# A decoder trunk whose first products take raw transposed tokens, the row norm applied at eviction

## The chip, the cores and the metric

The kernel runs on one core of one Trainium2 chip. The core has a matrix engine (TensorE, PE in the profile, with its weight loads as PEld), a vector engine (VectorE, DVE), a scalar engine (ScalarE, ACT), GpSimd (POOL) and a queue engine (SyncE, SP) that issues most of the DMAs. The metric is the device time of one execution in microseconds; lower is better. The time shown for a kernel is the median of several runs.

## The reference

A trunk of two pre-norm layers on 256 tokens of width 1024, all in float32. In each layer the RMS-normalised tokens go through one wide input projection, whose columns feed three causal mixers (a Mamba-2 scan, a sliding-window attention with sinks, a forgetting attention). Each mixer's output is projected, weighted by a sigmoid gate, summed, projected again and added to the stream. A last RMSNorm closes the trunk.

```
def rms_norm(x, w):
    y = x * lax.rsqrt(jnp.mean(x * x, axis=-1, keepdims=True) + NORM_EPS)
    return y * w

for layer in range(2):
    h = rms_norm(x, norm_w[layer])
    proj = h @ w_in[layer]            # 12832 columns
    (a_xbc, a_z, a_dt, b_q, b_k, b_v, b_z, c_q, c_k, c_v, c_f, c_z, gates) = split(proj)
    y_a = mamba2_branch(a_xbc, a_z, a_dt, ...)
    y_b = sliding_window_branch(b_q, b_k, b_v, b_z, sinks[layer], cos, sin)
    y_c = forgetting_attention_branch(c_q, c_k, c_v, c_f, c_z, f_bias[layer])
    branch = [y_a @ w_proj[layer, 0], y_b @ w_proj[layer, 1], y_c @ w_proj[layer, 2]]
    merged = sum(sigmoid(gates_i + gate_bias[layer, i]) * branch[i])
    x = x + merged @ w_out[layer]
return rms_norm(x, final_norm_w)
```

Note that a row's factor rsqrt(mean(x²)+eps) is one number per token. It can be applied to the tokens before a product or to the product's rows after it.

## The kernel before

**Products.** TensorE's fast float32 form takes rounded operands, so each operand is split: a high part (a rounded copy, written by ScalarE) and a low part (the remainder, original minus high, usually by VectorE). Every product is three passes: high by high, low by high, high by low (`dense`, line 273). The tokens are kept transposed as `hTh` and `hTl`, [128, 2 row tiles of 128 tokens, 8 slices of the width, 128].

**Weights.** The weight matrices are cut into pieces (256 or 512 columns) and these into parts of 512 KB, in one stream. `load_to` (line 327) issues the DMAs of parts on SP into six `raw` buffers. `feed` (line 358) splits parts, up to four ahead of the product in hand (`AHEAD`), into six `hi` and six `lo` buffers; `release` calls it as a product finishes with a part. One narrow piece of 32 columns (dt and the forget gate) has a buffer of its own.

**Order.** `ops` is a list of operations written out by hand. Layer 0 starts with k and v of the window attention (256 columns each, two parts each), then two q pieces of 512 columns (four parts each), then the narrow piece, the gate piece z, and the convolution pieces ("heavy") with lighter ones between (`lights`): two c_v pieces, gates, output projections. Attention and scan work is launched as generators with a delay in estimated TensorE time, and `pump` puts ready steps between products; `drain` forces one branch's steps out. TensorE runs in the written order throughout (`manual_schedule`). In the first section of the program, up to the v products, VectorE, ScalarE and GpSimd do as well; behind it a planner orders those engines. SP's queue is ordered by the planner too; `pin` keeps an instruction in written order on its engine.

**Banks.** Wide products take three banks (`pmm`), the rest, transposes among them, five (`pmx`).

**The start** (lines 1134 to 1181). SP loads x rows 0-127, the norm weight copied to all partitions, x rows 128-255, and the parts; GpSimd loads the rope table. Thirty transposes of the identity occupy TensorE (`WARM`). For the first row tile the squares are summed, the row factor is made (`row_rstd`: GpSimd's power and four small VectorE steps), x is multiplied by factor and weight (line 1160), transposed and split (`to_hT`). The second row tile goes through GpSimd and ScalarE and is transposed in the middle of the first k product (`second_rows`, through `after`). Two parts are split in halves by ScalarE with VectorE or GpSimd taking the remainder (lines 1148 and 1149).

**The constants** of a layer (`layer_consts`, line 403) are nine small DMAs in layer 0, issued on ScalarE's queue after the v products.

**The end** (`out_end`, line 988). For the last columns: add the residual (VectorE), square and sum (ScalarE), multiply by the final norm weight (VectorE), add to the variance (line 1003), power on GpSimd, two small VectorE steps, and then VectorE scales columns 0 to 511 and ScalarE 512 to 1023, each followed by its own DMA.

Of the kernel before, what the change touches and what calls it, by code (L numbers as in the profile page):

```python
# [16 lines left out]
P = 128  # L17
# [12 lines left out]
N_RAW, N_SPLIT = 6, 6  # L30
AHEAD = 4
WARM = 30
# [11 lines left out]
def hybrid_trunk(  # L44
# [110 lines left out]

    tab = T("tab", [P, 1])
# [3 lines left out]
    nwb0 = T("nwb", [P, D])  # L160
    nc.sync.dma_start(x0[:, 0, :], x2[0:P, :])
    nc.sync.dma_start(nwb0, norm_w[0:1, :].to_broadcast([P, D]))
    nc.sync.dma_start(x0[:, 1, :], x2[P:S, :])
# [26 lines left out]
    nc.gpsimd.dma_start(rope_sb, rope_tab.rearrange("(t p) c d -> p t c d", p=P))  # L190
# [82 lines left out]
    def dense(pt, ah, al, bh, bl, w, after=None, mid=None):  # L273


        passes = ((ah, bh), (al, bh), (ah, bl))
# [4 lines left out]
        for i, (k, a, b) in enumerate(seq):  # L281
            mm(pt, a(k), b(k), start=(i == 0), stop=(i == len(seq) - 1))
            if after is not None:
                if i % 12 == 11:
                    after[i // 12]()
# [28 lines left out]
    raws, pieces, pieces_out = {}, {}, {}  # L314

# [11 lines left out]
    def load_to(j):  # L327

        while state["load"] < min(j, len(stream)):
            i, k = stream[state["load"]]  # L330
            src, n = subs[i]
            kper = min(NK, 1024 // n)
            raw = T("raw" if n > 32 else "L1", [P, kper, n])
            for c, ap in src:
                m = ap.shape[-1]
                nc.sync.dma_start(raw[:, :, c:c + m],
                                  ap.rearrange("(k p) c -> p k c", p=P)[:, k:k + kper, :])
            raws[state["load"]] = raw
            state["load"] += 1
# [59 lines left out]
    y0.nwb = nwb0  # L399

    pdma = pin(nc.scalar.dma_start)

    def layer_consts(y):
        l = y.l
        vr = T("vr", [88, P])
# [36 lines left out]
    def tok(ah, al, w, t, turn=True, mid=None, **kw):  # L442
# [3 lines left out]
        p = pmm()  # L446
# [13 lines left out]
    def rope(p, t):  # L460

        p4 = p.rearrange("p (h d) -> p h d", h=4)
        cos = bc(rope_sb[:, t, 0, :], 1, 4)
        a = T("L1", [P, 4, 64])
        tt(a, p4, cos, op=ALU.mult)
        b = T("L1", [P, 4, 64])
        tt(b[:, :, 0:32], p4[:, :, 32:64], bc(rope_sb[:, t, 1, 0:32], 1, 4), op=ALU.mult)
        tt(b[:, :, 32:64], p4[:, :, 0:32], bc(rope_sb[:, t, 1, 32:64], 1, 4), op=ALU.mult)
        return a, b

    def u_bkv(y, c0, t, after=None):

        def f(w):
            p = tok(y.hTh, y.hTl, w, t, turn=w.n == 512 or c0 > 0, after=after)
            if t == 0 and c0 == 0:
                kv = T("L8", [P, 2048])
                y.kT = kv[:, 0:1024].rearrange("p (h s) -> p h s", h=4)
                y.bv = kv[:, 1024:1536].rearrange("p (t c) -> p t c", t=2)
            if c0 > 0:
                act(halves(y.bv[:, t, :]), p, AF.Copy)  # L480
            elif w.n == 512:
                act(y.bv[:, t, :], p[:, 1, :], AF.Copy)
            if c0 == 0:
                a, b = rope(p if w.n == 256 else p[:, 0, :], t)
# [3 lines left out]
                launch(1, rest(kd), D_K)  # L488
# [10 lines left out]
    def u_bq(y, c0, t):  # L499

        def f(w):
            p = tok(y.hTh, y.hTl, w, t, turn=w.n == 512)
            for i in range(w.n // 256):
                if t == 0:
                    y.qT[c0 + i] = T("qt", [P, 2, S])
                a, b = rope(p if w.n == 256 else p[:, i, :], t)
                q = T("L1", [P, 4, 64])
                gtt(q, a, b, op=ALU.add)
                launch(1, rest(c0 + i, q.rearrange("p h d -> p (h d)")), D_Q)
# [90 lines left out]
    def swa_quad(y, c, qT):  # L600
        yield lambda: (1, 0) in y.zdone
# [220 lines left out]
    def u_cv(y, c, t):  # L822
        def f(w):
# [3 lines left out]
            act(halves(y.cv[:, t, c:c + w.n]), p, AF.Copy)  # L827
# [160 lines left out]
    def out_end(y, c, t, i, n, xo, p):  # L988
        sl = slice(c, c + n)
        with tc.high_priority():  # L990
            tt(halves(y.xn[:, t, sl]), p, halves(xo), op=ALU.add)
            sum_sq(y.xn, t, c, y.ss[t][:, i:i + 1], n)
            last = y.l + 1 == L
            nwb = fin["w"] if last else layers[y.l + 1].nwb
            if last:
                stt(y.xn[:, t, sl], y.xn[:, t, sl], -0.5, nwb[:, sl], op0=ALU.mult, op1=ALU.mult)
# [4 lines left out]
            if i == 2:  # L1001
                v = y.var[t][:, 1:2]
                stt(v, y.ss[t][:, 2:3], 1.0 / D, y.var[t][:, 0:1], op0=ALU.mult, op1=ALU.add)
                r = row_rsqrt2(v)
                if last:
                    ts(y.xn[:, t, 0:512], y.xn[:, t, 0:512], r[:, 0:1], None, op0=ALU.mult)
                    nc.sync.dma_start(out2[t * P:(t + 1) * P, 0:512], y.xn[:, t, 0:512])
                    act(y.xn[:, t, 512:D], y.xn[:, t, 512:D], AF.Copy, scale=r[:, 0:1])  # L1008
                    nc.scalar.dma_start(out2[t * P:(t + 1) * P, 512:D], y.xn[:, t, 512:D])
# [34 lines left out]
    for y in layers:  # L1044
        l = y.l
        w = w_in[l]
        y.gate, y.qT, y.ckT, y.sz, y.yh, y.yl, y.sq, y.h, y.ss, y.var, y.zdone, y.cqdone = {}, {}, {}, {}, {}, {}, [], {}, {}, {}, set(), {}
# [11 lines left out]
        def gates_proj(br):  # L1059
# [4 lines left out]
            def p(b):  # L1064
                c = 512 * b
                if b == 0 and br != 0:
# [34 lines left out]
        lights = [lambda: None, lambda: op(cols(C_CV, 512), u_cv(y, 0, 0), u_cv(y, 0, 1))]  # L1101
        lights += [lambda: None, lambda: op(cols(C_CV + 512, 512), u_cv(y, 512, 0), u_cv(y, 512, 1))]
# [114 lines left out]
```

## Time and profile before

| | before |
|---|---|
| median of 3 runs | 848.63 us (848.49 to 848.87) |
| profiled execution, its time | 847.65 us |
| its span, first to last instruction | 845.9 us |
| mean granted TensorE clock | 0.996 |
| TensorE busy | 833.4 us, 99% |
| VectorE busy | 642.3 us, 76% |
| ScalarE busy | 511.6 us, 60% |

The span is shorter than the time by 1.75 us, which lies around the first and last instruction. Rows of a timeline read: start, duration, engine, line, operation, what it writes and reads with shapes, a count, and in brackets the engine's idle time just before and what ended it. The chain of work is followed back from the last instruction; its rows are start, duration and what it was. Rows of waits read: who waited for whom, total us, times, longest. Rows by window read: the stretch, its length, then busy us and count of PE, PEld, DVE, ACT and POOL, the granted clock as a share of full speed, the DMA engines' busy share, and GB/s. A TensorE row that counts as busy can still run at a lower clock.

### The profile page before, as it was taken

The numbers are of one execution on the slowest core, as the hardware profiler recorded it, in microseconds if no ns is written. First come the engines' busy times: TensorE is split into PE (matmuls) and PEld (weight loads), VectorE is DVE, ScalarE is ACT, GpSimd is POOL, SyncE is SP. The second block draws the span as 40 slices with busy tenths as digits, with TensorE's granted clock in tenths as the row PEclk, the third lists the DMA queues.
The fourth block names the chain that finished last, engine by engine and source line by source line (L and its number), as shares of the span: only waits on it lengthen the run. The fifth ranks groups of instructions, "written<-read, shape, count | busy, mean of one in ns | idle before, by whom it ended". The sixth has DMA issues, their size and how long they took to land.

```text
span 845.9 us, 15985 instructions
## 1 busy us (share of the span) xinstructions
PE 833.4 (99%) x5964; PEld 763.3 (90%) x5964; DVE 642.3 (76%) x1403; ACT 511.6 (60%) x1004; POOL 104.5 (12%) x134
## 2 busy tenths in 40 slices
PE   7999999999999999999999999999999999999996
PEld 7999898989999998888989998899899999988896
DVE  5777997998776679656788879879968667785665
ACT  6466777665666667435555667776557667654442
POOL 6310100000131010210014001000003110121000
PEclk9999999999999999999999999999999999999999
DMA  8666565666465545648676465465755555576632
GB/s 303 183 205 208 166 200 162 201 210 197 128 202 175 172 159 187 218 155 282 206 237 218 143 206 159 142 199 183 241 171 176 174 175 152 161 235 212 212 100 76
DMA packets 126638, 158.43 MB, mean 187 GB/s; under 512 B 12784, under 2 KB 88224, under 8 KB 126560
## 3 DMA queue, kind: packets, MB, share of 16 engines
q1 hardware_dynamic: 109456, 140.79, 52.9%
q10 hardware_dynamic: 17056, 16.49, 6.4%
q8 instruction: 47, 0.77, 0.4%
q14 instruction: 31, 0.25, 0.1%
q0 software_dynamic: 48, 0.13, 0.0%
HBM read 155.22 MB, written 2.16 MB: 186 GB/s over the span
## 4 chain that ended last, share of the span: by engine, by line
PE 95%; DMA 2%; ACT 0%; DVE 0%; issue 0%; POOL 0%; SPq 0%; POOLq 0%; DVEq 0%; ACTq 0%
PE mm L96 82%; PE mx L96 9%; PE mx L100 4%; DMA raw<-in_w_proj_dram 2%; DMA raw<-in_w_in_dram 1%; POOL lo L1149 0%; ACT hi L1148 0%; ACT hi L259 0%; ACT L L1008 0%; DVE L L260 0%; DVE L L935 0%; DVE L L934 0%; ACT L L259 0%; POOLq L1213 0%; ACT L L215 0%
## 5 line engine op out<-in xcount | busy, mean ns | idle before, releaser
L260 DVE TENSOR_TENSOR lo<-raw,hi 128x1024 fp32r<-128x1024 f32 x252 | 308.2, 1234 | 94.9 <-ACT hi L259 81.9
L96 PE MATMUL mm<-hi,L 128*128 128x512 f32 (+1 forms) x1344 | 373.9, 364 | 1.9 <-ACT hi L1148 1.4
L259 ACT ACTIVATE hi<-raw 128x1024 fp32r<-128x1024 f32 x252 | 263.2, 1056 | 93.0 <-PE mm L96 66.9
L96 PE MATMUL mm<-L,hi 128*128 128x256 f32 x1792 | 317.7, 278 | 0.0
L96 PEld LDWEIGHTS mm<-L,hi 128*128 128x128 f32 x1792 | 277.7, 192 | 6.8 <-issue 3.3
L96 PEld LDWEIGHTS mm<-hi,L 128*128 128x128 f32 x1344 | 241.5, 190 | 32.4 <-issue 2.7
L96 PE MATMUL mm<-L,lo 128*128 128x256 f32 x896 | 246.4, 275 | 0.0
L96 PE MATMUL mm<-lo,L 128*128 128x512 f32 (+1 forms) x672 | 241.3, 360 | 0.6 <-POOL lo L1149 0.6
L96 PEld LDWEIGHTS mm<-L,lo 128*128 128x128 f32 x896 | 171.9, 192 | 0.2
L96 PEld LDWEIGHTS mm<-lo,L 128*128 128x128 f32 x672 | 127.3, 190 | 15.4 <-POOL lo L1149 0.8
L862 POOL TENSOR_SCALAR_AFFINE_SELECT bias<-bias 128x128 f32<-128x128 f32 x64 | 35.7, 593 | 407.8 <-DMA bias<-cumd 232.7
L556 ACT ACTIVATE pp<-pp,nm 128x128 f32<-128x128 f32 (+1 forms) x128 | 56.5, 443 | 13.0 <-DVE nm L550 13.0
L693 DVE SCALAR_TENSOR_TENSOR L<-L,vec,L 128x255 f32<-128x255 f32 (+2 forms) x96 | 46.3, 482 | 4.8 <-ACT L L690 3.4
L96 PE MATMUL mx<-L,L 128*64 128x128 f32 (+1 forms) x384 | 34.4, 314 | 0.0
L886 ACT ACTIVATE L<-L 128x512 f32<-128x512 f32 x24 | 15.2, 632 | 30.2 <-DVE L L885 30.0
L568 DVE TENSOR_SCALAR pp<-pp,rsum 128x128 f32<-128x128 f32 (+1 forms) x128 | 32.1, 314 | 0.5
L696 ACT ACTIVATE L<-L 128x256 f32<-128x256 f32 x32 | 13.3, 417 | 31.4 <-DVE L L693 25.9
L96 PEld LDWEIGHTS mx<-L,L 128*64 128x64 f32 x384 | 22.9, 136 | 9.4 <-ACT pp L556 1.3
L777 ACT ACTIVATE L<-mm 128x256 f32<-128x256 f32 x48 | 18.1, 378 | 21.0 <-PE mm L96 21.0
L585 ACT ACTIVATE L<-mx 128x512 f32<-128x512 f32 x48 | 27.0, 596 | 2.7 <-PE mx L100 2.5
L100 PE MATMUL mx<-ident,pp 128*128 128x128 f32 x192 | 26.3, 273 | 0.0
L100 PE MATMUL mx<-ident,L 128*128 128x128 f32 x152 | 23.1, 279 | 1.6 <-DVE L L935 0.8
(173 smaller groups left out, 716.0 us busy)
## 6 DMA issues: line engine op xcount, KB each, us to landing
raw<-in_w_in_dram SPq DMA_DIRECT2D x200, 512.0 KB, 4.3
raw<-in_w_proj_dram SPq DMA_DIRECT2D x48, 512.0 KB, 5.6
raw<-in_w_out_dram SPq DMA_DIRECT2D x16, 512.0 KB, 5.1
L<-cumd ACTq DMA_DIRECT2D x8, 512.0 KB, 5.2
bias<-cumd ACTq DMA_DIRECT2D x16, 256.0 KB, 3.8
L<-in_gate_bias_dram ACTq DMA_DIRECT2D x12, 256.0 KB, 3.9
L<-in_x_dram SPq DMA_DIRECT2D x2, 512.0 KB, 5.0
nwb<-in_norm_w_dram SPq DMA_DIRECT2D x1, 512.0 KB, 5.4
```

The lines of the kernel that those rows point to most:

```text
L96: nc.tensor.matmul(o, a, b, **kw)
L100: nc.tensor.transpose(o, a, i)
L259: keep(act)(hi, src, AF.Copy)
L260: keep(tt)(lo, src, hi.bitcast(F32), op=ALU.subtract)
L556: act(pp[:, i, sl], pp[:, i, sl], AF.Exp, scale=-1.0, bias=nm[:, e:e + 1], accum_out=sums[:, e:e + 1])
L568: ts(pp[:, i, sl], pp[:, i, sl], rs[:, 2 * i + b:2 * i + b + 1], 0.5, op0=ALU.mult, op1=ALU.mult)
L585: act(pT, pt, AF.Copy)
L693: stt(a[:, s:S], x_[:, 0:S - s], y.vec[:, 16 * j + u:16 * j + u + 1], a[:, s:S], op0=ALU.mult, op1=ALU.add)
L696: act(th, a, AF.Tanh)
L777: act(halves(th), p, AF.Tanh, scale=0.5)
L862: nc.gpsimd.affine_select(out=bias[:, i, dst], in_=bias[:, i, src], compare_op=ALU.is_ge, fill=NEG, base=0, pattern=[[-1, P]], channel_mul ...
L886: act(g, g, AF.Tanh, scale=0.5)
```

## The change

In layer 0 the first products (k, v, both q pieces and the first c_v piece) take x transposed and multiplied by the norm weight, without the row factor. The factor is applied where these products leave their banks: in the rope steps of k and q, and as the scale of the copies of v and c_v. The norm weight arrives as an [8, 128] block on ScalarE's queue and is transposed once, instead of the copy to all partitions.

The k evictions are kept back (`late`) until after the v products, since the factor exists only then; the first k tile gets a bank from the other pool. After the q pieces a new step `normalize` broadcasts the factor by two small products and multiplies the stored transposed tokens by it, splitting them into new `hTh` and `hTl`, which everything from the narrow piece on uses. For this the first c_v piece moves ahead of the narrow piece; the lighter pieces between the heavy ones are placed anew in layer 0, and the split of the window attention's output is placed two operations earlier.

SP's queue is reordered: x rows 0-127 in two halves, part 0 in two halves, part 1, x rows 128-255, the rope table (from GpSimd's queue), then parts 2 to 5. The constants of layer 0 are issued by SP when the stream reaches part 8, no longer by ScalarE. The narrow piece is loaded when the stream is eight parts short of it, in both layers. The thirty transposes at the start become ten, with ten more before the first product.

At the end of the last layer the last squares are summed on VectorE, the variance step comes ahead of the multiplication by the norm weight, and the last scaling is divided at column 640.

```diff
-WARM = 30
+EARLY = 8
+WARM = 10
+FILL = 10
...
+    nw8 = T("L1", [NK, P])
+    nc.scalar.dma_start(nw8, norm_w[0:1, :].rearrange("o (k p) -> (o k) p", p=P))
...
-    nc.sync.dma_start(x0[:, 0, :], x2[0:P, :])
-    nc.sync.dma_start(nwb0, norm_w[0:1, :].to_broadcast([P, D]))
-    nc.sync.dma_start(x0[:, 1, :], x2[P:S, :])
+    for j in range(2):
+        nc.sync.dma_start(x0[:, 0, j * 512:(j + 1) * 512], x2[0:P, j * 512:(j + 1) * 512])
...
+    def load_part(j):
+        i, k = stream[j]
+        ...
+        step_ = kper // 2 if j == 0 else kper
+        ...
+    def load_to(n_):
+        while state["load"] < min(n_, len(stream)):
+            j = state["load"]
+            for e in range(j, min(j + EARLY, len(stream))):
+                if subs[stream[e][0]][1] == 32 and e not in raws and e >= state["split"]:
+                    load_part(e)
+            if j == 8:
+                layer_consts(y0, nc.sync)
+            if j not in raws:
+                load_part(j)
+            state["load"] += 1
...
+        for o, i, r in ((a, p4, rope_sb[:, t, 0, :]),
+                        (b[:, :, 0:32], p4[:, :, 32:64], rope_sb[:, t, 1, 0:32]),
+                        (b[:, :, 32:64], p4[:, :, 0:32], rope_sb[:, t, 1, 32:64])):
+            if y.rn is None:
+                tt(o, i, bc(r, 1, 4), op=ALU.mult)
+            else:
+                stt(o, i, y.rn[:, t:t + 1], bc(r, 1, 4), op0=ALU.mult, op1=ALU.mult)
...
-            p = tok(y.hTh, y.hTl, w, t, turn=w.n == 512 or c0 > 0, after=after)
+            p = tok(y.hTh, y.hTl, w, t, turn=w.n == 512 or c0 > 0, after=after,
+                    bank=pmx if after and t == 0 else pmm)
+            end()
...
+            (late.append if after is not None else lambda g: g())(lambda: evict(w, p))
...
-                act(halves(y.bv[:, t, :]), p, AF.Copy)
+                act(halves(y.bv[:, t, :]), p, AF.Copy, scale=y.rn[:, t:t + 1])
...
-            sum_sq(y.xn, t, c, y.ss[t][:, i:i + 1], n)
+            if last and i == 2:
+                nc.vector.tensor_tensor_reduce(out=junk[:, 0:n], in0=y.xn[:, t, sl], in1=y.xn[:, t, sl], ...)
+            else:
+                sum_sq(y.xn, t, c, y.ss[t][:, i:i + 1], n)
+            if i == 2:
+                v = y.var[t][:, 1:2]
+                pin(stt)(v, y.ss[t][:, 2:3], 1.0 / D, y.var[t][:, 0:1], op0=ALU.mult, op1=ALU.add)
             if last:
-                stt(y.xn[:, t, sl], y.xn[:, t, sl], -0.5, nwb[:, sl], op0=ALU.mult, op1=ALU.mult)
+                pin(stt)(y.xn[:, t, sl], y.xn[:, t, sl], -0.5, nwb[:, sl], op0=ALU.mult, op1=ALU.mult)
...
+                    m = 640
...
-            op(k, u_bkv(y, 0, 0, [lambda j=j: second_rows(j) for j in range(2)]))
-            op(k, u_bkv(y, 0, 1))
+            op(k, u_bkv(y, 0, 0, {16: lambda: second_rows(0), 20: lambda: second_rows(1)}, lambda: first_end()))
+            op(k, u_bkv(y, 0, 1, {}))
             op(v, u_bkv(y, 256, 0), u_bkv(y, 256, 1))
-            op(None, lambda: layer_consts(y0))
             for c in (0, 2):
                 op(cols(C_BQ + 256 * c, 512), u_bq(y, c, 0), u_bq(y, c, 1))
+            op(None, lambda: launch(9, normalize(y0), 0.0))
+            op(cols(C_CV, 512), u_cv(y, 0, 0), u_cv(y, 0, 1))
+            op(None, lambda: normalized(y0))
...
+        if l == 0:
+            lights = {2: [lambda: cv(512)], 4: [gp.pop(0)], 6: [lambda: op(None, lambda y=y: split_late(y, 1))],
+                      7: [gp.pop(0)]}
+        else:
+            lights = {1: [lambda: cv(0)], 3: [lambda: cv(512)], 4: [gp.pop(0)], 6: [gp.pop(0)]}
...
+    def normalize(y):
+        rb = T("L1", [P, S])
+        for t in range(2):
+            act(rb[:, t * P:(t + 1) * P], ident, AF.Copy, scale=y.rn[:, t:t + 1])
+        yield 2.0
+        p = pmx()
+        for t in range(2):
+            mm(p[:, t * P:(t + 1) * P], ones, rb[:, t * P:(t + 1) * P], start=True, stop=True)
+        hTh = T("L8", [P, 2, NK, P], F32R)
+        hTl = T("L8", [P, 2, NK, P], F32R)
+        for t in range(2):
+            for k in (0, 4):
+                xk = xw[:, t, k:k + 4, :]
+                tt(xk, xk, bc(p[:, t * P:(t + 1) * P], 1, 4), op=ALU.mult)
+                split(hTh[:, t, k:k + 4, :], hTl[:, t, k:k + 4, :], xk)
...
+        load_to(2)
+        nc.sync.dma_start(x0[:, 1, :], x2[P:S, :])
+        nc.sync.dma_start(rope_sb, rope_tab.rearrange("(t p) c d -> p t c d", p=P))
         load_to(N_RAW)
...
+        square(0, 0)
+        turn(0, 0)
+        w_high(parts[0], 0)
+        high(0, 0)
+        turn(0, 1)
+        for i in range(FILL):
+            transpose(warm[:, 0:P], ident, ident)
+        low(0, 0)
+        w_high(parts[0], 2)
+        w_low(parts[0], 0)
+        w_low(parts[0], 2, gtt)
+        high(0, 1)
+        w_high(parts[1], 0)
+        low(0, 1)
+        w_low(parts[1], 0)
+        w_high(parts[1], 2)
+        w_low(parts[1], 2, gtt)
+        square(0, 1)
+
+        def second_rows(j):
+            turn(1, j)
+
+        def first_end():
+            high(1, 0)
+            high(1, 1)
+            low(1, 0)
+            low(1, 1)
+            w_high(parts[2], 0)
+            w_high(parts[2], 2)
+            w_low(parts[2], 2, gtt)
+            w_low(parts[2], 0)
+            w_high(parts[3], 0)
+            w_high(parts[3], 2)
+            w_low(parts[3], 0)
+            square(1, 0)
+            square(1, 1)
+            w_low(parts[3], 2)
+            ...
+            y0.rn = rsqrt(v, 2)
```

Here `turn` transposes four slices of x and multiplies them by the norm weight (VectorE), `high` and `low` split the tokens (ScalarE, VectorE), `w_high` and `w_low` split half a weight part (`gtt` is GpSimd), and `square` sums squares on ScalarE.

More of the change, by code (lines that the diff above doesn't have):

```diff
@@ new lines, in square @@
+        def square(t, j):
+            sum_sq(x0, t, 512 * j, ss[:, 2 * t + j:2 * t + j + 1], 512)
+        parts = [new_part() for _ in range(4)]
+        square(0, 0)
[12 more added lines that the diff above has]
+        low(0, 1)
@@ L1182, in hybrid_trunk @@
     with tc.manual_schedule(engines={ENG.PE}):
+        for g in late:
+            g()
         for i, f, last in ops[3:]:
```

157 lines of the change are left out of this document (76 added, 81 removed).

## The prediction

> **What bounds the kernel now.** I read the page's busy shares first, then who waited for whom on TensorE, then the chain of work over the first 27 us, then the timelines of both ends.
>
> ```profile
> PE 833.4 (99%) x5964; PEld 763.3 (90%) x5964; DVE 642.3 (76%) x1403; ACT 511.6 (60%) x1004; POOL 104.5 (12%) x134
> PE mm L96 <- ACT hi L1148: 1.4, 1, 1.4
> PE mx L100 <- DVE L L935: 0.8, 1, 0.8
> PE mm L96 <- POOL lo L1149: 0.6, 1, 0.6
> ```
>
> TensorE is busy 99% of 845.9 us. Its longest wait after the start is 0.8 us. Time can be won at the two ends only: before products run densely, and after the last one.
>
> ```profile
> 2.18 7.77 DMA raw<-in_w_in_dram
> 9.98 1.16 ACT hi L1148 x2
> 11.20 1.78 POOL lo L1149
> 13.02 0.80 PE mm L96 x2
> 17.36 8.36 PE mm L96 x72
> ...
> 10.66 1.50 PE L96 MATMUL mm<-hi,L 128*128 128x256 f32 x8 [1.38 <-ACT hi L1148]
> ...
> 25.56 0.60 PE L100 MATMUL mx<-ident,L 128*128 128x128 f32 x4
> ...
> 13.00:16.00 3.00, 2.98 (x14) 2.98 (x15) 0.60 (x2) 1.58 (x4) 2.90 (x2) 0.50 1.06 381
> 16.50:17.00 0.50, 0.50 (x7) 0.50 (x6) 0.50 (x2) 0.43 (x1) 0.00 (x0) 1.00 1.05 389
> ```
>
> The start waits for the first weight part: it lands at 9.95, fourth in SP's queue behind three transfers of 512 KB. Then come its rounding on ScalarE and its remainder on GpSimd. After that sparse stretch the granted clock is 0.50 from 13.0 to about 16.3. The four k and v products end at 25.56 (my mark), where the first q product follows; from there TensorE hardly stops. So the change is worth what it moves this mark, plus the tail, plus new waits.
>
> **The start, step by step.** These rows give the durations:
>
> ```profile
> 0.80 0.39 SPq L161 DMA_DIRECT2D L<-in_x_dram  x1
> 4.47 0.63 ACT L215 ACTIVATE L<-L 128x512 f32<-128x512 f32 x1 [2.18 <-DMA L<-in_x_dram]
> 8.03 0.63 ACT L215 ACTIVATE L<-L 128x512 f32<-128x512 f32 x1 [2.83 <-DMA L<-in_x_dram]
> 9.27 0.57 ACT L259 ACTIVATE L<-mx 128x512 fp32r<-128x512 f32 x1
> 9.88 0.69 DVE L260 TENSOR_TENSOR L<-mx,L 128x512 fp32r<-128x512 f32 x1
> 11.20 1.76 POOL L1149 TENSOR_TENSOR lo<-raw,hi 128x512 fp32r<-128x512 f32 x1 [0.83 <-ACT hi L1148]
> 14.61 1.29 POOL L1149 TENSOR_TENSOR lo<-raw,hi 128x512 fp32r<-128x512 f32 x1
> 5.78 0.57 POOL L203 TENSOR_TENSOR sm<-sm,mhalf 128x1 f32<-128x1 f32 x1 [1.59 <-DVE sm L220]
> 6.38 0.16 DVE L205 TENSOR_TENSOR sm<-sm 128x1 f32<-128x1 f32 x1 [0.76 <-POOL sm L203]
> 25.61 1.04 ACT L259 ACTIVATE hi<-raw 128x1024 fp32r<-128x1024 f32 x1
> 28.89 1.21 DVE L260 TENSOR_TENSOR lo<-raw,hi 128x1024 fp32r<-128x1024 f32 x1
> 1.52 3.70 PEld L100 LDWEIGHTS mx<-ident 128*128 128x128 f32 x18 [1.52 <-POOL ident masks.py:199]
> 7.96 0.42 PEld L100 LDWEIGHTS mx<-ident,L 128*128 128x128 f32 x4 [0.94 <-DVE L L1160]
> ```
>
> Landings. Before, the 1st, 3rd and 4th half megabyte were there at 4.47, 8.03 and 9.95, so the 2nd at about 6.2. The new queue holds x rows 0-127 (two halves), part 0 (two halves), part 1, x rows 128-255, the rope table, parts 2 to 5. By position: half of x at 3.5, half of part 0 at 5.4, all of it at 6.3, part 1 at 8.0, second x rows at 9.7; parts 2 and 3 at 11.4 and 12.8. SP issues three transfers more in front (two halves, the rope table that GpSimd issued), at 0.39 each as for x; by 5.3 all are out, and bytes, not issue, set the landings. The small norm-weight transfer, first on ScalarE's queue, lands under the ten warm-up transposes, cost 0.
>
> First row tile of k. Four transposes of raw x (0.42), DVE's multiplication by the norm weight (0.69): 5.2. ScalarE rounds half of part 0 (5.4 to 6.0), then the tokens (0.57): 6.6. The ten filling transposes behind the second four (5.2) take 1.9 at the slow pace of the PEld row and end at about 7.1, so the first product starts there, against 10.66 before. The last needs part 1's second half: 8.0, two roundings (9.1), GpSimd's remainder of 1.3 to 1.8: 10.4 to 10.9. With the eight transposes of the second x rows between them, these 24 products end at 11.2.
>
> Second row tile. DVE multiplies until 11.55, ScalarE rounds until 12.2, DVE takes remainders until 12.95. 24 products at 8.36/72 = 0.116 us, one wait of 0.5: 14.5. v: 48 products, whose parts 2 and 3 are split by 15.4: 14.5 + 5.4 = 19.9. The mark moves by **-5.7 us** (ends: -7.0 if everything lands a microsecond earlier, -3.5 if the late half is a microsecond later and TensorE loses clock).
>
> The removed stall has a successor, the rstd. Its squares end on ScalarE at 15.9; two small DVE steps, GpSimd's 0.57 and four DVE steps of 0.16, each with its hand-over, end at 17.9. Queued behind them on DVE, in the written order, stand the remainders of the four parts of the first q piece (1.21 each): 19.2, 20.4, 21.6, 22.8. The q product asks for the first at 20.3 and then one every 1.3 us, so there is 1.1 us to spare: cost 0, and one for one beyond that. The k evictions, put off to behind these, run on DVE until about 25; nobody waits for their keys before the attention quads, near 54.
>
> **Normalising the stored tokens.** Two matrix products for the broadcast:
>
> ```profile
> L96 PE MATMUL mx<-L,ones x32: 272/275/275, 313.2 to 745.7; 128*128 128x128 f32 x32
> 48.71 4.43 PE mm L96 x40
> ...
> 46.00:60.00 14.00, 14.00 (x118) 13.02 (x117) 10.98 (x42) 9.14 (x30) 2.30 (x2) 1.00 0.92 295
> 60.00:110.00 50.00, 50.00 (x410) 45.90 (x408) 43.53 (x127) 35.48 (x89) 3.29 (x8) 1.00 0.56 171
> ```
>
> 2 x 0.275 = **+0.5 us** of TensorE. Behind them: four multiplications and four remainders on DVE (8 x 0.69 = 5.5) and four roundings (2.3). They can start after the first row tile of the c_v piece, at about 48.1. The first product on the normalised tokens, the narrow one, comes 5.8 later (48.7 before, less 5.7, plus 10.4 for the moved c_v piece, plus 0.5 = 53.9). Interleaved well this ends at 53.7; with every hand-over waited for, four times 2.05, at 56.3. I take **+0.8 us**; ends 0 and what the third rival gives.
>
> The scale in the evictions costs nothing on ScalarE, and about 0.1 us per rope on DVE, which was busy 11.0 of 14 us there. Taking c_v ahead leaves the following convolution stretch denser. It has 43.5 us of DVE in 50 (second row above, DVE is the third pair); a piece of 10.4 us TensorE and 4.9 us DVE leaves, giving 38.6 in 39.6. Full, but parts are split four ahead, 10 us of cover: cost 0, up to +4 if that cover is used up. The earlier split of the attention output stays at the same total of work ahead of it: 0.
>
> **Constants and narrow piece.**
>
> ```profile
> 33.60 0.60 ACT L495 ACTIVATE L<-mx 128x512 f32<-128x512 f32 x1 [5.24 <-DMA hb<-in_dt_bias_dram]
> dsk<-in_d_skip_dram ACTq DMA_DIRECT2D x4, 2.0 KB, 8.7
> ```
>
> ScalarE gets back 5.24 us, which no product waited for: 0. On SP the nine constants stand ahead of part 8 and the two narrow transfers (and TensorE is 5.7 us earlier). Each waits for one of a few outstanding transfers, as the old ones did on ScalarE; I estimate part 8 issued at about 20 and landed between 24 and 28.7 (with the 8.7 us of the d_skip row). Two steps of 1.04 and 1.21 make 31 at the latest. TensorE wants it at 19.9 + 10.4 + eight transposes = 31.1. Cost 0, up to +3. The Trainium skill, "DMA: Bandwidth & Descriptors", section "Queues, rings and completion order", says that a DMA engine takes turns between queues, a packet at a time, but keeps ring order in one: by this, weight parts no longer slip between the constants, which makes the late end likelier, 846.6 instead of 843.6. No row of before can show it. The narrow piece was not waited for by TensorE: 0.
>
> **The tail.**
>
> ```profile
> 5.09 0.08 DVE L1154 DVE_READ_ACCUMULATOR2_ANT ss<- 128x1 f32 x1
> ...
> 839.05 0.42 DVE L991 TENSOR_TENSOR L<-mm,L 128x256 f32<-128x256 f32 x1 [0.25 <-PE mm L96]
> 839.51 0.42 ACT L215 ACTIVATE L<-L 128x256 f32<-128x256 f32 x1 [1.69 <-DVE L L991]
> 840.05 0.43 DVE L996 SCALAR_TENSOR_TENSOR L<-L,nwb 128x256 f32<-128x256 f32 x1 [0.57 <-ACT L L215]
> 840.39 0.15 DVE L1003 SCALAR_TENSOR_TENSOR sm<-ss,sm 128x1 f32<-128x1 f32 x1
> 840.68 0.56 POOL L226 TENSOR_TENSOR sm<-sm,mhalf 128x1 f32<-128x1 f32 x1 [7.28 <-DVE sm L1003]
> 841.73 0.49 DVE L1006 TENSOR_SCALAR L<-L,rs 128x512 f32<-128x512 f32 x1
> 841.73 0.72 ACT L1008 ACTIVATE L<-L,rs 128x512 f32<-128x512 f32 x1 [1.71 <-DVE rs L230]
> ```
>
> From the sum (839.05) to the variance step takes 1.34. Now the square stays on DVE (0.42 and a read of the sum, 0.08, no hand-over) and the 0.43 multiplication falls behind the variance step, under GpSimd's 0.56: about 0.8, so -0.55. ScalarE's last scaling shrinks from 512 to 384 columns: 0.72 to about 0.6. DVE's grows to 640 columns, 0.6. **-0.6 us** (ends -0.3, -0.8).
>
> **Sum.** -5.7 + 0.5 + 0.8 - 0.6 = -5.0: a span of 840.9, and 842.6 for the profiled run, which took 847.65. That run is 1.0 below the median of the three timed ones, 848.63; carried over to it, **843.6 us**.
>
> **Rivals.** (1) *The clock falls.* The PEld rows (weight loads) show 18 transposes at 206 ns and, after nothing but transposes, four at 105: they raise the pace. Fewer of them, with gaps where x is late, may leave the first products at half clock for one stretch as from 13.0 to 16.3: 3.3 us at half rate is +1.7, 845.3. Against it: TensorE is occupied nearly throughout from 1.5. The Trainium skill, "TensorE: Matmul & The Clock Gate", section "Part 4: PE-mode transpose", says that transposes do not count as activity for the full clock; by this rule 845.3 would be the forecast, but the two rows speak against it.
>
> (2) *The change doesn't start q earlier.* Three banks take the wide products: second k tile, both v tiles. If the first q tile gets the bank of k, it waits for a put-off eviction behind four remainders on DVE, until about 24.8: +4.9, 848.5. For it: k's bank was filled first. Against: v's first bank is free at about 18.4.
>
> (3) *Slower: the normalised tokens come late.* The narrow product needs both row tiles. If DVE first takes four waiting remainders (4.9) and then each step with its hand-over (8.2), it ends at 61.2: 7.3 us of wait, and, as after the sparse start, 1.7 of half clock. Sum -5.7 + 0.5 + 9.0 - 0.6 = +3.2: 851.8. It outweighs the gain from 5.8 us of loss on. Against it: DVE was idle 3 of 14 us there, and these steps are issued ahead of the next parts.
>
> (4) *Part 8, or DVE in the denser stretch, is late:* +3, 846.6.
>
> **Chances.** Forecast 0.58 (841.8 to 845.2); (1) 0.12; (2) 0.12; (3) 0.10; (4) 0.08. The range 841.8 to 848.3 leaves out (3), half of (2) and a little below. 0.2% (1.7 us) is about what a measurement tells from no change: faster is the forecast, (1), (4) and a share of (2), 0.81; same 0.07; slower 0.12.
>
> **What would show it.** In the profile after: first product at about 7, end of v near 20, no half clock; the q product following without a wait; TensorE's wait ahead of the narrow product under 2 us; the tail from last product to end 0.6 shorter. A new wait of several microseconds on TensorE before 60 us, or 0.50 in the clock column, would make the forecast wrong.

## The result

| | before | after |
|---|---|---|
| median of the runs | 848.34 us (847.40 to 848.87, 6 runs) | 853.42 us (852.74 to 856.88, 6 runs) |
| profiled execution: its time, its span | 847.65, 845.9 us | 853.25, 851.5 us |
| mean granted clock | 0.996 | 0.992 |

The changed kernel is slower: ratio 1.0067, 95% interval 1.0049 to 1.0085. The forecast was 843.6 us, with 848.3 as its upper end.

From the page of the changed kernel, the busy line:

```profile
PE 833.0 (98%) x5959; PEld 762.2 (90%) x5959; DVE 650.5 (76%) x1411; ACT 511.4 (60%) x1006; POOL 97.2 (11%) x129
```

Its waits of TensorE, total us, times and longest:

```profile
PE mm L98 <- ACT L L500: 7.8, 1, 7.8
...
PE mx L98 <- DVE lo L1234: 0.9, 1, 0.9
PE mm L98 <- ACT L L1222: 0.5, 1, 0.5
...
```

One wait of 7.8 us is new; the longest in the kernel before, after the start, was 0.8. Its place in the chain of work (start, duration, what):

```profile
2.69 5.41 DMA raw<-in_w_in_dram
...
11.99 7.03 DMA raw<-in_w_in_dram
...
20.48 12.58 DMA raw<-in_w_in_dram
...
34.63 7.90 PE mm L98 x24
```

Before, the chain left the transfers at 9.95 us and stayed with TensorE from 13.02 on. Now a weight transfer holds it until 33.06. TensorE's timeline, with the first product, the first q product, the stop and what follows it:

```profile
6.98 1.51 PE L98 MATMUL mx<-hi,L 128*128 128x256 f32 x8
...
21.50 0.60 PE L98 MATMUL mm<-hi,L 128*128 128x512 f32 x2
...
26.47 0.38 PE L98 MATMUL mm<-lo,L 128*128 128x512 f32 x1
34.63 1.22 PE L98 MATMUL mm<-hi,L 128*128 128x512 f32 x2 [7.78 <-ACT L L500]
...
39.78 0.60 PE L98 MATMUL mm<-hi,L 128*128 128x512 f32 x2
40.21 0.38 PE L98 MATMUL mm<-lo,L 128*128 128x512 f32 x1
40.43 0.59 PE L98 MATMUL mm<-hi,L 128*128 128x512 f32 x2
```

The k and v products end, and q's begin, at 21.50; before, k and v ended at 25.56: 4.1 us are won. The second row tile of q should start at 26.9 and starts at 34.63. It wants a bank, and the bank still holds v's second tile, whose eviction is ScalarE's L500. ScalarE's timeline says why that is late:

```profile
19.59 0.47 ACT L500 ACTIVATE L<-mm,rs 128x256 f32<-128x256 f32 x1
...
33.16 1.06 ACT L260 ACTIVATE hi<-raw 128x1024 fp32r<-128x1024 f32 x1 [12.16 <-DMA raw<-in_w_in_dram]
34.12 0.46 ACT L500 ACTIVATE L<-mm,rs 128x256 f32<-128x256 f32 x1
```

v's first tile is evicted at 19.59. In front of the second eviction the planner has placed the rounding (`hi`) of weight part 8. ScalarE waits 12.16 us for that part, and the eviction, which needs nothing from it, waits behind it. SP's queue and the DMAs (issue to landing, median us):

```profile
12.45 0.88 SPq L255 DMA_DIRECT2D vr<-in_conv_w_dram  x1
...
19.04 1.32 SPq L255 DMA_DIRECT2D dsk<-in_d_skip_dram  x2
20.48 0.55 SPq L338 DMA_DIRECT2D raw<-in_w_in_dram  x1
```

```profile
dsk<-in_d_skip_dram SPq DMA_DIRECT2D x2, 2.0 KB, 9.7
```

```profile
19.50:29.50 10.00, 7.35 (x44) 6.33 (x42) 5.96 (x10) 1.51 (x3) 5.06 (x4) 0.99 0.06 5
30.00:39.00 9.00, 4.37 (x10) 3.53 (x11) 4.19 (x8) 3.84 (x5) 0.41 (x1) 0.50 1.04 363
```

Part 8 is issued at 20.48, just behind the two small d_skip transfers. In the first stretch of the last fence all DMA engines together move 5 GB/s, with 0.06 of sixteen engines busy (less than one). Its first microsecond had no weight part to move; for the other nine part 8 was waiting. In the second stretch 363 GB/s flow. Part 8 lands at 33.06. The stop also costs clock: it is 0.50 from 30 to 39. Three products take 0.65 us at full clock (39.78 to 40.43); the twelve from 34.63 to 39.78 take 5.15 where four times 0.65 is 2.6, so **2.55 us** more.

The account of the profiled runs: -4.1 (first q product) + 7.8 (wait) + 2.55 (half clock) + 0.4 (normalising: four matmuls from 60.10 to 60.47) = +6.65. Near 330 us the lag is 6.4 (the same stretch of 36 products starts at 323.40 before and at 329.83 after), at the last long stretch 5.8 (820.38 and 826.18), and the spans differ by 5.6. The microsecond between 6.65 and 5.6 I didn't follow.

### The profile page after: what moved, and what is told of

It is laid out like the page before. It is cut to its first block, busy times and chain, and to the rows that moved or that the text cites. A ratio compares the mean times of both kernels' runs of the same rounds, so it can differ in the third digit from the quotient of the medians.

```text
span 851.5 us, 15966 instructions
## 1 busy us (share of the span) xinstructions
PE 833.0 (98%) x5959; PEld 762.2 (90%) x5959; DVE 650.5 (76%) x1411; ACT 511.4 (60%) x1006; POOL 97.2 (11%) x129
## 4 chain that ended last, share of the span: by engine, by line
PE 93%; DMA 4%; issue 1%; DVE 1%; ACT 0%; SPq 0%; POOL 0%; POOLq 0%; DVEq 0%; ACTq 0%
PE mm L98 79%; PE mx L98 9%; PE mx L102 4%; DMA raw<-in_w_in_dram 3%; DMA raw<-in_w_proj_dram 1%; POOL lo L1234 0%; SPq L338 0%; SPq L255 0%; ACT hi L1230 0%; ACT hi L260 0%; DVE lo L261 0%; SPq L165 0%; DVE L L261 0%; DVE L L955 0%; DVE L L954 0%
## 5 line engine op out<-in xcount | busy, mean ns | idle before, releaser
L882 POOL TENSOR_SCALAR_AFFINE_SELECT bias<-bias 128x128 f32<-128x128 f32 x64 | 32.8, 549 | 413.3 <-DMA bias<-cumd 152.5
L716 ACT ACTIVATE L<-L 128x256 f32<-128x256 f32 x32 | 13.4, 418 | 30.8 <-DVE L L713 27.2
L605 ACT ACTIVATE L<-mx 128x512 f32<-128x512 f32 x48 | 26.9, 596 | 1.3 <-PE mx L102 1.1
L570 DVE CUSTOM_DVE_ANT_0 pp<-mx,wmask,nsink 128x128 f32<-128x128 f32 x64 | 23.8, 413 | 1.5 <-PE mx L98 1.5
```

The costliest lines, as they stand in the source:

```text
L570: nc.vector.tensor_tensor_reduce(out=pp[:, i, sl], in0=score(p, i, b), in1=biases(p, i, b), scale=-0.125, scalar=1.0e30 if ns is None else ...
L605: act(pT, pt, AF.Copy)
L882: nc.gpsimd.affine_select(out=bias[:, i, dst], in_=bias[:, i, src], compare_op=ALU.is_ge, fill=NEG, base=0, pattern=[[-1, P]], channel_mul ...
```

## The experiments

The theory after reading these traces: the 4-byte pieces of d_skip (every second value, one for each of 64 partitions, twice) bring all weight transfers to a standstill for about ten us; moved to SP in front of part 8 they delay it, and the eviction behind its rounding makes TensorE wait. The rivals: the other constants or SP's order alone; the bank; the tail, the narrow piece or the start.

**The constants back behind v, everything else as changed.**

```diff
-            if j == 8:
-                layer_consts(y0, nc.sync)
...
+            op(None, lambda: layer_consts(y0, nc.scalar))
```

> The changed kernel with one part undone: the nine constants of layer 0 go back to ScalarE's queue, after the v products. Theory A (the constants ahead of part 8 on SP make it land at 33.1; its rounding stands ahead of the second v eviction on ScalarE, so the second q tile waits 7.8 us for a bank and then runs 5 us at half clock): part 8 lands before 25, the wait for the v eviction falls below 0.5 us, no half clock, about 843 us (853.4 - 7.8 - 2.6). Rival B (the new start, the put-off evictions or the normalising step cost the time, and the constants only show up as the last of several waits): still above 849 us, with a wait of 4 us or more somewhere before 60 us.

Measured: 843.88 us (843.12 to 844.66), ratio to before 0.994 (0.9919 to 0.9962). The wait of 7.8 is gone, and nothing over 0.6 us takes its place. So the move of the constants turned a gain of 4.4 us into a loss of 5.1.

**Only the d_skip transfers later.** The other seven constants stay in front of part 8; the two d_skip transfers go in front of part 24.

```diff
+            if j == 24:
+                y0.skips()
...
```

> The changed kernel; seven constants stay on SP ahead of part 8, only the two d_skip transfers (elements of 4 bytes) are issued later, ahead of part 24. Theory A4 (it is d_skip alone that stops the weight transfers for some ten microseconds): part 8 lands within 5 us of its issue, no wait for the v eviction, 843 to 846 us, and the stretch without transfers reappears behind part 23. Rival N (nine small transfers, each waiting for an earlier one, are what delays part 8): part 8 still lands after 28, wait of 3 us or more, 848 us or more.

Measured: 842.84 (842.72 to 843.56), ratio 0.9929 (0.9903 to 0.9954). Part 8 is in time. The standstill has moved with the transfers (a row by stretch, columns as above):

```profile
50.00:52.00 2.00, 2.00 (x12) 1.79 (x11) 1.71 (x3) 1.52 (x3) 0.00 (x0) 1.00 0.05 0
```

At 50 us TensorE stays busy through it, with parts that had landed before. The standstill belongs to d_skip, and it costs where the parts in hand don't cover it.

**d_skip as one row.** One transfer brings all sixteen values (64 bytes) to each partition; two GpSimd copies of 0.2 us each pick every second one. Both layers.

```diff
+        dall = T("dall", [P, 16], bufs=2)
+        pdma(dall, d_skip[l:l + 1, :].to_broadcast([P, 16]))
...
-            src = d_skip[l:l + 1, :].rearrange("o (j two) -> two o j", two=2)[half]
-            pdma(y.dsk[64 * half:64 * half + 64, :], src.to_broadcast([64, NK]))
+            hs = slice(64 * half, 64 * half + 64)
+            nc.gpsimd.tensor_copy(y.dsk[hs, :], dall[hs, :].rearrange("p (j two) -> p two j", two=2)[:, half, :])
```

> The changed kernel with d_skip loaded as a copy of its 64-byte row to every partition (one transfer, like the other heads' constants) and picked apart by two small GpSimd copies, in both layers; all constants stay on SP ahead of part 8. Theory A4: no stretch without transfers before 40 us, no wait for the v eviction, 842 to 844 us. Rival N: the delay stays, since the count of transfers on SP falls only from nine to eight: 848 us or more.

Measured: **841.92 (841.69 to 842.34), ratio 0.9918 (0.9887 to 0.9948)**: faster than both kernels. Its DMA row, and the stretch that held the standstill:

```profile
dall<-in_d_skip_dram SPq DMA_DIRECT2D x1, 8.0 KB, 2.8
```

```profile
19.50:29.50 10.00, 10.00 (x57) 8.98 (x56) 9.89 (x15) 5.57 (x9) 7.55 (x6) 1.00 0.93 305
```

One transfer with twice the bytes of the two together lands in 2.8 us, where each of the two took 9.7, and 305 GB/s flow where 5 did. TensorE is busy for the ten us without a gap. The constants stay on SP here, so SP's order alone isn't the cause.

**Is it the piece size?** The changed kernel, two transfers as before, each of eight neighbouring values in place of every second one. So 14 of the 16 skips get the value of another head (the expectation below says half of them).

```diff
-            src = d_skip[l:l + 1, :].rearrange("o (j two) -> two o j", two=2)[half]
+            src = d_skip[l:l + 1, NK * half:NK * half + NK]
```

> The changed kernel, with each of the two d_skip transfers reading eight neighbouring values (32 bytes in a row) in place of every second one (4 bytes each): two transfers on SP ahead of part 8 as before, the same bytes, another value in half of the skips. Theory E (the standstill is made by the 4-byte pieces): the transfers land in about 2 us, part 8 lands by 26, no 7.8 us wait, time 841.7 to 843. Rival B (it is made by broadcasting to the partitions, or by anything else of these two transfers): one of sixteen DMA engines stays busy alone for 8 to 10 us, part 8 lands about 33, time 852.5 to 854.5.

Measured: 842.35 (842.14 to 842.94), ratio 0.9928 (0.9915 to 0.9941). The d_skip row of its DMA view, and the stretch that held the standstill:

```profile
dsk<-in_d_skip_dram SPq DMA_DIRECT2D x2, 2.0 KB, 2.3
```

```profile
19.50:29.50 10.00, 10.00 (x57) 8.98 (x56) 8.64 (x13) 5.25 (x8) 6.07 (x4) 1.00 0.82 260
```

The same bytes, count of transfers, queue and place: only the pieces are 32 bytes instead of 4, and so an eighth as many. The packet lines of the changed kernel and of this one:

```profile
DMA packets 126894, 157.91 MB, mean 185 GB/s; under 512 B 12808, under 2 KB 88768, under 8 KB 126816
```

```profile
DMA packets 125102, 157.91 MB, mean 188 GB/s; under 512 B 11016, under 2 KB 86976, under 8 KB 125024
```

1792 packets fewer for two layers is 896 for each, which is 1024 pieces of 4 bytes less 128 pieces of 32. That settles what makes the standstill: the small pieces. Why pieces that keep less than one of sixteen engines busy hold up all other transfers, no run shows. The Trainium skill, "DMA: Bandwidth & Descriptors", section "Rules for kernel authors", states that a strided last dimension becomes one descriptor per element; the packet counts agree.

**Does it take the same queue?** In the kernel before, d_skip was on ScalarE's queue, and SP had weight parts under way: it issued one at 33.09, one at 36.43 and one at 37.56. The stretch there, then that of the kernel before with d_skip as one row:

```profile
34.00:39.50 5.50, 5.50 (x28) 4.78 (x27) 4.32 (x7) 3.99 (x5) 0.19 (x2) 1.00 0.06 4
```

```profile
34.00:39.50 5.50, 5.18 (x25) 4.19 (x23) 4.64 (x7) 3.65 (x4) 1.14 (x4) 1.00 0.53 157
```

4 GB/s with the pieces, 157 without them: the weights were stopped by another queue's transfer too. The prediction cites a rule for this from the Trainium skill, "DMA: Bandwidth & Descriptors", section "Queues, rings and completion order": a DMA engine takes turns between queues. Here that didn't keep the weights going. In the kernel before TensorE didn't wait for them.

> The kernel before with d_skip alone changed: one row of 64 bytes to every partition and two small GpSimd copies. Before, the weight transfers stand still from about 33.5 to 39.5 us. Theory A4: that stretch goes away, but no product waited for it, so the time stays within 0.3% of before. Rival H (the standstill was paid for somewhere later): 846 us or less.

Measured: 847.68 (847.39 to 849.61), ratio 0.9993 (0.9984 to 1.0002): no difference that can be told, as a hidden stop must give. (In this kernel the two GpSimd copies wait for the row and TensorE waits 1.6 us for GpSimd behind them, so the hidden stop could have been worth as much.)

**The kernel before, with nothing but the constants moved to SP in front of part 8.**

```diff
+            if state["load"] == 8:
+                layer_consts(y0, nc.sync)
...
-            op(None, lambda: layer_consts(y0))
...
```

> The kernel before with one part of the change alone: the nine constants issued by SP ahead of part 8. Theory A (part 8's rounding ahead of v's second eviction in ScalarE's order, whatever the start): part 8 lands near 37, the second q tile waits 6 to 9 us and then runs at half clock, 856 to 861 us. Rival S (it hurts only because the new start has TensorE 4 us further on): 851 us or less.

Measured: 855.25 (854.41 to 856.25), ratio 1.008 (1.0063 to 1.0096). SP's queue and TensorE's timeline:

```profile
19.65 2.09 SPq L254 DMA_DIRECT2D dsk<-in_d_skip_dram  x2
21.86 9.08 SPq L338 DMA_DIRECT2D raw<-in_w_in_dram  x4
```

```profile
42.68 0.44 PE L100 MATMUL mx<-ident,L 128*128 128x128 f32 x2 [2.04 <-POOL L L509]
44.34 0.69 PE L100 MATMUL mx<-ident,L 128*128 128x128 f32 x2 [1.22 <-POOL L L509]
44.68 1.20 PE L96 MATMUL mm<-hi,L 128*128 128x512 f32 x2
```

Without any raw tokens the move alone costs 7 us. Here the eviction waits only 0.5 us; the price is paid through VectorE, whose rope steps stand behind the late remainders, then GpSimd's rope sums, then half clock (1.20 for two products, 0.59 at full clock). The place differs, the cause is the same late part 8 (its rounding waits 12.62 us for the transfer). The wait of 6 to 9 us at q's second tile that I expected here didn't come, and the time lies just under the 856 to 861 that I gave.

**Is the bank the cause?** The changed kernel with v's second tile in the other pool, so that the second q tile needn't wait for its eviction.

```diff
-                    bank=pmx if after and t == 0 else pmm)
+                    bank=pmx if (after and t == 0) or (y.l == 0 and c0 > 0 and t == 1) else pmm)
```

> The changed kernel with one bank moved: the second v tile goes to the pool of five banks, so the second q tile finds a free wide bank. Constants as in the changed kernel. Theory A (the wait is for the bank whose eviction stands behind part 8's rounding on ScalarE): the 7.8 us wait goes; instead the first product of the second q piece, due near 32.5, waits for part 8's remainder at about 35.5, 2 to 3 us, and the clock stays up or falls for less: 845 to 848 us. Rival C (the wait is for part 8 itself, whatever the banks): 852 us or more.

Measured: 855.28 (854.04 to 855.88), ratio 1.0071 (1.0044 to 1.0099). The wait of 7.8 is gone, and the time is not. TensorE now waits for part 8's own rounding (1.5) and remainder (0.6), and then for GpSimd (TensorE's row, then GpSimd's), with the clock at 0.50 again from 44 to 48:

```profile
43.89 0.69 PE L102 MATMUL mx<-ident,L 128*128 128x128 f32 x2 [3.61 <-POOL L L528]
```

```profile
39.93 3.91 POOL L528 TENSOR_TENSOR L<-L,L 128x256 f32<-128x256 f32 x1 [0.18 <-DVE L L483]
```

The 845 to 848 that my theory gave was missed, and the time lies where the rival had it (852 or more): the theory took the bank for the only link. Any step queued in order behind the late part serves as well, here the rope steps on VectorE. What stops is the part, and removing one of those who wait for it moves the wait on.

**The narrow piece in its turn** (on top of the one-row kernel).

```diff
-EARLY = 8
+EARLY = 1
```

> The changed kernel with d_skip by rows, and the narrow piece loaded in its turn instead of eight parts early. Prediction's term, 0: within 0.5 us of the run with d_skip by rows (841.9). Rival E (the early load keeps the narrow product from waiting): 843 us or more, with a wait of TensorE ahead of the narrow product near 56 us.

Measured: 841.78 (841.71 to 842.09), against 841.92: loading it early is worth nothing, as forecast.

**The new tail in the kernel before**, no other edit (the squares on VectorE, the variance step ahead, the division at 640, as in the change's diff).

> The kernel before with the end of the changed kernel alone (last squares summed on VectorE, variance step first, last scaling divided at column 640). The prediction's term: 0.6 us faster, 847.7. The trace of the changed kernel: last transfer issued 0.46 us earlier but landing later, since VectorE's share is larger, 0.2 us faster, 848.1.

Measured: 848.18 (846.91 to 850.98), ratio 0.9998 (0.9988 to 1.0009): between nothing and what can't be told from it, not -0.6.

**GpSimd beside VectorE at the start** (on top of the one-row kernel): three weight remainders from GpSimd to VectorE.

```diff
-        w_low(parts[0], 2, gtt)
+        w_low(parts[0], 2)
...
-        w_low(parts[1], 2, gtt)
+        w_low(parts[1], 2)
...
-            w_low(parts[2], 2, gtt)
+            w_low(parts[2], 2)
```

> The kernel with d_skip as one row, and the three weight remainders of the start that GpSimd takes (8, 10 and 15 us) given to VectorE too. Theory (VectorE's 512-column remainder takes 1.79 and 1.77 us only because GpSimd works beside it): VectorE's six remainders between 6.8 and 11.5 us take 0.7 us each, so the work that ended at 11.5 ends at about 10.9 although VectorE does all of it; the first product's waits shrink, q starts 0.5 to 0.8 us earlier than with GpSimd's help, time 841.1 to 841.6. Rival (the long remainder is VectorE's own, for instance its source being written at that time): the remainders stay at 1.8 us, VectorE has 2.5 to 3.5 us more to do ahead of k's second tile, time 843.5 to 845.

Measured: 844.62 (843.2 to 846.75), ratio 0.9955 (0.9941 to 0.997). VectorE in the changed kernel, GpSimd in the changed kernel, and VectorE in this one:

```profile
7.57 1.79 DVE L1234 TENSOR_TENSOR lo<-raw,hi 128x512 fp32r<-128x512 f32 x1
...
9.89 1.77 DVE L1234 TENSOR_TENSOR lo<-raw,hi 128x512 fp32r<-128x512 f32 x1
...
14.17 0.69 DVE L1234 TENSOR_TENSOR lo<-raw,hi 128x512 fp32r<-128x512 f32 x1
```

```profile
7.53 1.29 POOL L1234 TENSOR_TENSOR lo<-raw,hi 128x512 fp32r<-128x512 f32 x1 [4.20 <-ACT hi L1230]
9.35 1.77 POOL L1234 TENSOR_TENSOR lo<-raw,hi 128x512 fp32r<-128x512 f32 x1 [0.53 <-ACT hi L1230]
```

```profile
7.50 1.52 DVE L1236 TENSOR_TENSOR lo<-raw,hi 128x512 fp32r<-128x512 f32 x2
...
9.79 1.29 DVE L1236 TENSOR_TENSOR lo<-raw,hi 128x512 fp32r<-128x512 f32 x2 [0.17 <-ACT hi L1232]
```

The durations went as the theory had it: two remainders take 1.52 and 1.29 on VectorE alone, less than one beside GpSimd. VectorE's step from 7.57 ends 0.54 after GpSimd's (8.82), its step from 9.89 ends 0.54 after the next (11.12): as if it had waited for GpSimd to finish and then run its own 0.69. The Trainium skill, "SBUF — State Buffer", section "Who interferes with whom", says that a VectorE step with two inputs in SBUF contends with a GpSimd step that reads SBUF, and that issue order decides which of them is blocked. The rows agree. The time, though, lies in the range that I gave the rival (843.5 to 845), and not by the rival's mechanism. SP's order, which the planner makes, came out otherwise: both narrow transfers ahead of two parts, the constants from 16.9 us on (12.4 in the one-row kernel), part 8 rounded at 28.2 (23.6), and TensorE waits 2.7 us for v's evictions. So this run shows what made the remainders long, and not what giving them to VectorE would bring.

**Without the ten filling transposes** (on top of the one-row kernel: `FILL = 0`).

> The kernel with d_skip as one row, without the ten filling transposes ahead of the first product (5.54 to 6.79 us); nothing else. Theory K (they keep the clock): the idle time of TensorE before the first product, 1.1 us, comes on top of the 0.95 and 0.52 us of waits behind it, and a granted clock of 0.5 shows for 3 to 5 us between 9 and 17 us, as it did in the kernel before from 13 us; time 843.5 to 844.5. Rival N (transposes do not count for the clock, and the filled time was a wait anyway): the clock stays at 1.00 or is low in both, the first product stays at 6.9 us, time 841.6 to 842.3.

Measured: 842.68 (842.11 to 844.21), ratio 0.9935 (0.9923 to 0.9947), against 0.9918 for the one-row kernel; the intervals overlap. TensorE with the fillers, then without:

```profile
5.54 1.25 PE L102 MATMUL mx<-ident 128*128 128x128 f32 x10
6.86 1.48 PE L98 MATMUL mx<-hi,L 128*128 128x256 f32 x8
```

```profile
6.73 2.17 PE L98 MATMUL mx<-hi,L 128*128 128x256 f32 x8 [0.71 <-ACT L L1224]
9.16 1.22 PE L98 MATMUL mx<-lo,L 128*128 128x256 f32 x4 [0.26 <-DVE lo L1236]
```

Without them eight products take 2.17 instead of 1.48, the half pace lasts until 13.4, and k's second tile begins at 13.93 instead of 12.86. The clock column doesn't show it. The same microsecond with the fillers, then without:

```profile
10.00:11.00 1.00, 1.00 (x11) 1.00 (x10) 1.00 (x1) 0.00 (x0) 0.99 (x1) 1.00 1.10 348
```

```profile
10.00:11.00 1.00, 1.00 (x6) 1.00 (x6) 1.00 (x1) 0.00 (x0) 0.85 (x1) 1.00 1.11 357
```

Eleven matmuls against six, and 1.00 in the column both times. So the place and number that I gave (0.50 in the column from 9 us) were wrong, and the time lies between the two expectations.

How much of this is due to the fillers stays open, because the moment when the pace rises differs between traces with the same start. Here the ten fillers take 1.25 us; with the constants back they take 2.13, and in the last kernel below 2.34. All nine traces with fillers are at full pace by about 8 us, the one without at 13.4. What the row at 5.54 does show is that work of nothing but transposes raised the pace: ten take 1.25 us there, ahead of any product, where the first ten of this kernel took 2.39. The Trainium skill, "TensorE: Matmul & The Clock Gate", section "Part 4: PE-mode transpose", says that transposes don't engage the full clock; the prediction set this rule aside, and these rows don't bear it out.

**The constants behind v, and one row.**

> The changed kernel with the constants issued from ScalarE behind v's products, as before, and d_skip as one row: the move of the constants undone and the 4-byte pieces gone. With the pieces and the old place (constants back) the first narrow product came at 56.8 and the time was 843.9; with rows and the new place it came at 55.6 and the time was 841.9. Theory P (the 2 us between them are the pieces' standstill, moved to 32 to 40 us; the place of the constants is worth nothing by itself): narrow product at 55.4 to 55.9, time 841.6 to 842.4. Rival Q (they are the nine issues on ScalarE's queue and the later landing of the constants): narrow product at 56.5 or later, time 843.2 to 844.2.

The edits are those of the first and the third experiment together. Measured: 842.72 (841.83 to 845.98), ratio 0.9933 (0.9914 to 0.9951): neither expectation. Its profiled execution took 845.79, 3 us above that median, and GpSimd shows why:

```profile
33.19 0.43 POOL L431 COPY dsk<-dall 64x8 f32<-64x8 f32 x2 [4.75 <-DMA dall<-in_d_skip_dram]
33.70 5.38 POOL L528 TENSOR_TENSOR L<-L,L 128x256 f32<-128x256 f32 x4
```

My own copies wait 4.75 us for the row, q's rope sums stand behind them, and TensorE waits 2.0 us for those. Behind that wait the clock falls to 0.50 and twelve products take 4.36 us (37.95 to 42.31) where 2.6 is full pace. Together that is 3.8 of the 4.0 us by which this span, 844.0, exceeds that of the one-row kernel. It explains this execution, not the median. Whether the place of the constants is worth anything once the pieces are gone stays open: this trace shows the price of the copies.

## Why the prediction was wrong

**Constants, "cost 0, up to +3": the step that failed.** I had part 8 issued at 20 and landed between 24 and 28.7. It was issued at 20.48 and landed at 33.06. I took the d_skip row's 8.7 us for the delay of a transfer of its own, and let part 8 run beside it; in the trace nothing runs beside it, and part 8 moves only when it ends, near 29.5. The row that would have told was in the trace of before, the 4 GB/s from 34 to 39.5: I read the landing time and not the DMA share beside it. Price: 7.8 of wait and 2.55 of half clock, where the worst end was 3. With the pieces gone, as rows of 32 or of 64 bytes, the time is 842.35 or 841.92, inside the forecast's own range.

**"Who waits for that", the second fault of the same step.** I asked when q's products need part 8 (31.1). But the first to wait was v's eviction, queued behind part 8's rounding on ScalarE, and through its bank q's second tile, at 26.9. Rival (2) named the bank, for the first q tile and k's eviction on VectorE; the bank was the second tile's, and the eviction v's on ScalarE. Rival (4) named the late part, and gave it +3. Neither saw that the two were one chain.

**The mark, -5.7: right in mechanism, measured -4.1.** v took 5.35 (forecast 5.4), and there was no half clock at 13 to 16 us. The first product came at 6.98 (7.1), in part by luck: the fillers began at 5.66 instead of 5.2 and took 1.25 instead of 1.9. (Ten at the 206 ns of the row would be 2.06.) The first row tile of k was the term that was off, about 1.2 us too short: VectorE's remainders take 1.79 and 1.77 beside GpSimd, where I had 0.69 (the experiment on the start). The second tile began at 12.98, after a wait of 0.5 as forecast, and took 3.17 where 24 products at 0.116 are 2.8.

**Normalising, +0.5 and +0.8.** The broadcast shows as four matmuls that take 0.37 us, and the narrow product had no wait: 0 for the 0.8. Rival (3), which needed 7 us there, fell.

**The tail, -0.6.** The scaling started 2.32 us after the sum, before 2.68:

```profile
844.84 0.42 DVE L1011 TENSOR_TENSOR L<-mm,L 128x256 f32<-128x256 f32 x1 [0.25 <-PE mm L98]
...
847.16 0.55 DVE L1034 TENSOR_SCALAR L<-L,rs 128x640 f32<-128x640 f32 x1
```

From the sum to the end of the span it is 6.66 us after and 6.85 before, -0.2; done alone, nothing that can be told.

**Rival (1), the clock.** Not at the first products: the pace was up by 5.66, when the fillers ran in 1.25 us. The last experiment but one shows that without fillers it can fail there, as this rival feared. The half clock came later, from the stop.

**The narrow piece, 0, and ScalarE's 5.24 us, 0:** right; the first was tried, and the second shows in no wait of TensorE.

**The sum without the standstill.** The one-row kernel has a span of 840.0; the forecast was 840.9. That it comes so near is luck, for its terms are further off: the mark is 1.5 short (21.40 in this kernel), while the 0.8 for the narrow product and a wait of 0.8 near 387 us fell away, and about another microsecond is spread over the layers, which I didn't follow.

## What to carry to other kernels

Before a small DMA is moved in front of work that somebody waits for, look at the DMA share and the GB/s during its landing, not only at its landing time: a transfer in pieces of one value each can stop everything, hidden only as long as parts are in hand. On an engine with an order, ask for each wait that grows late what stands behind it on the same queue; a step that needs nothing of the late data can be the first to hold TensorE. And when one waiting step is freed and the time stays, look upstream, at what is late, before freeing the next.

## What the hardware showed

- A broadcast of every second float, 1024 pieces of 4 bytes, moved almost nothing (0.06 of the engines, 5 GB/s from 19.5 to 29.5) and held the weight transfers of its own queue and of the other one. As pieces of 32 bytes it landed in 2.3 us instead of 9.7.
- VectorE's step of 0.69 took 1.79 us when GpSimd had started a step of the same kind just ahead; GpSimd's sum of 128x256, 0.73 elsewhere in the same kernel, took 3.91 where VectorE's remainders ran from 39.76 to 43.25 (the kernel with v's bank moved).
- Products can run at half pace while the clock column reads 1.00 (without fillers, six matmuls from 10 to 11 us instead of eleven): near the start the durations are the safer sign.
